# Token-major SSM operands by VectorE transposes of 32x32 squares and transfers through DRAM, in place of TensorE transposes

## The chip, the cores and the metric

The kernel runs on one core of a Trainium2 chip. The metric is the device time of one execution in microseconds; 3 timed runs of the kernel before have a median of 1086.67 us (1086.59 to 1087.11). The core has five engines that run their own instruction queues in order and wait for each other on semaphores: TensorE (PE in the profile; PEld is its weight load), VectorE (DVE), ScalarE (ACT), GpSimd (POOL) and SyncE (SP). SP and POOL also issue DMAs; 16 DMA engines carry them out.

## The reference, cut to what matters

One decoder layer on x of 512 tokens by 1024 channels, all float32: a normalised input projection, dilated attention and a Mamba-2 mixer side by side, gates, an output projection, and a squared-ReLU MLP. The change lies in the Mamba-2 mixer (8 groups, 4 heads of 64 channels each, state 128, chunks of 128 tokens):

```python
xbc = jax.nn.silu(conv(xbc) + conv_b)                 # depthwise, causal, 4 taps
xs, bm, cm = jnp.split(xbc, [SSM_INNER, SSM_INNER + SSM_GROUPS * SSM_STATE], axis=-1)
...
xd = (x * dt[..., None]).reshape(b, c, ch, g, hg, p)
cb = jnp.einsum('bclgn,bcsgn->bcgls', cc, bc)
y_diag = jnp.einsum('bcghls,bcsghp->bclghp', cb[:, :, :, None] * decay, xd)
states = jnp.einsum('bclgn,bcghl,bclghp->bcghpn', bc, decay_states, xd)
...
y_off = jnp.einsum('bclgn,bcghpn,bcghl->bclghp', cc, prev, jnp.exp(a_cs))
y = y + d_skip * xh;  y = y * silu(z);  y = y * rsqrt(mean(y * y) + eps) * norm_w   # per group
```

## The kernel before, in words

Every large matmul multiplies float32 numbers as a high and a low part (`split`, L95: ScalarE writes the high part, VectorE subtracts to get the low one), in three matmuls for each product (`three`). Weights come by SP DMAs into `ws_*`, and are split into `wh_*` and `wl_*`, two buffers of each.

The SSM stage runs over 8 groups g. For each group four kinds of projections are made as units of work that a filler hands to TensorE between the other steps: `x{g}` (PSUM tiles psx, two of 128 channels by 512 tokens), `bc{g}` (psbc: B, then C), `z{g}` (psz) and `sp{g-1}` (pssp: the projection of the group before to the model width, 8 tiles, each added to acc). After each psx or psbc tile `conv_silu` (L689) does the convolution on VectorE (ch, L693), a tanh on ScalarE (L696) and the last product on VectorE (ct, L697). The result has channels on partitions and tokens along the row.

`ssm_group` (L768) then has seven steps. In the first, x must have tokens on partitions: TensorE transposes it in eight 128x128 pieces into PSUM (ptx, through `tr`, L230), VectorE multiplies by dt into xd (L780), scales to xs, and splits it into xsh and xsl. In the second, B of the first three chunks is transposed likewise (pb) and split into bkh and bkl; TensorE multiplies B by C (pcb), VectorE masks it (cbm, L798) and multiplies the decays w (L802). The third step has the nine matmuls of the chunk states (pst, of bkh, bkl, xsh, xsl) and the running state prev. The fourth has pyd (xd and w) and pyo (prev and C) and forms y. The fifth takes the mean square of y (sq, pn, pnt, rt) and gives the row rstd to all partitions through DRAM: POOL writes rt_d (L859) and reads it back as rg (L861); it also starts the read of the next group's decays w (L754). In the last, y times nw and rg (L868) is split into yth and ytl for the projection sp{g}.

Between the steps the filler runs for a number of microseconds of TensorE work by its own count: `SSM_FILL` (L46) for groups 0 to 6, `SSM_LAST` for group 7. TensorE's instructions stand in the order of the program; those of VectorE, ScalarE, POOL and SP are put into an order by priorities, in which evacuations of projection tiles go ahead. The SSM tiles come from a pool in which tiles of one tag share buffers (sq has two, t1 two, xd one).

Of the kernel before, what the change touches and what calls it, by code (L numbers as in the profile page):

```python
# [11 lines left out]
F32 = mybir.dt.float32  # L12
F32R = mybir.dt.float32r
AF = mybir.ActivationFunctionType
ALU = mybir.AluOpType
# [3 lines left out]
P = 128  # L19
T = 512  # L20
NT = 4
# [16 lines left out]
UC = 256  # L38
# [4 lines left out]
BIG = 1e30  # L43

FILL0, FILL1, FILLA, FILLB, FILLC = 3.0, 4.0, 3.0, 2.8, 2.8
SSM_FILL = (2, 7, 4, 3, 10.5, 5, 4.5)  # L46
SSM_LAST = (3, 8, 4, 3, 9, 8, 8)

V_ORDER = tuple((d, i) for d in (1, 0, 2) for i in range(NT))
# [34 lines left out]
def hybrid_block(ctx: ExitStack, tc: tile.TileContext, a: dict):  # L84
    nc = tc.nc
    act, dve, pool, pe, sp = nc.scalar, nc.vector, nc.gpsimd, nc.tensor, nc.sync
# [5 lines left out]
    dram = ctx.enter_context(tc.tile_pool(name="dram", bufs=1, space=DRAM))  # L92


    def split(src, hi, lo, eng=None, pinned=False, lo_pinned=False):  # L95
        ins = act.activation(hi, src, AF.Copy)  # L96
        if pinned:
            tc.keep_in_program_order(ins)
        ins = (eng or dve).tensor_tensor(lo, src, hi.bitcast(F32), op=ALU.subtract)  # L99
        if lo_pinned:  # L100
            tc.keep_in_program_order(ins)
# [60 lines left out]
    def v3(t, k):  # L162
        return t.rearrange("p (k n) -> p k n", k=k)
# [65 lines left out]
    def tr(dst, src):  # L229
        tc.keep_in_program_order(pe.transpose(dst, src, ident))  # L230
# [27 lines left out]
    def abank(name):  # L258
        return psa.tile([P, T], F32, name=name, tag="a")
# [18 lines left out]
    with tc.tile_pool(name="start", bufs=1, reuse_waits="tile") as st:  # L278
# [163 lines left out]
        t = [vp.tile([P, GROUPS, NT, HG], F32, name=f"dt{j}") for j in range(4)]  # L442
# [22 lines left out]
    dtc = dtp.rearrange("p g c h -> p (g c h)")  # L465
# [50 lines left out]
    def in_unit(key, evac):  # L516

        hi, lo = take(key)
        for c in range(2):
            ps = gbank(f"ps{key}_{c}")  # L520
            yield from gemm_part(ps, v3(hi, KD), v3(lo, KD), c, range(KD), KD, uhk, ulk)
            with tc.high_priority(offset=400):
                evac(c, ps)
        done()
# [103 lines left out]
    for key in ATT_UNITS:  # L628
        n, j = key[:-1], int(key[-1])
        fill.add(key, qk_unit(n, j) if n in "qk" else z_unit(0, sz0) if n == "z" else gate_unit(n, j))  # L630
    fill.through("q0")
    pc, pa, pt = abank("pc"), abank("pa"), abank("pact")
# [51 lines left out]
    sg = sctx.enter_context(tc.tile_pool(name="ssm", bufs=1, side="right", reuse_waits="tile"))  # L684
# [4 lines left out]
    def conv_silu(ct, ps, tag, bufs):  # L689
        h = sg.tile([P, T], F32, name=f"ch{ct}", tag="ch", bufs=2)  # L690
        act.activation(h, ps, AF.Identity, bias=cb_[:, ct : ct + 1], scale=cw[:, ct, 3:4])  # L691
        for d in (1, 2, 3):
            dve.scalar_tensor_tensor(h[:, d:], ps[:, : T - d], cw[:, ct, 3 - d : 4 - d], h[:, d:],  # L693
                                     op0=ALU.mult, op1=ALU.add)
        t = sg.tile([P, T], F32, name=f"ct{ct}", tag=tag, bufs=bufs)
        act.activation(t, h, AF.Tanh)  # L696
        dve.scalar_tensor_tensor(t, t, 1.0, h, op0=ALU.add, op1=ALU.mult)  # L697
        return t

    def bc64(t, g, c0=0, c1=NT):  # L700
        v = t[:, g * 16 + c0 * HG : g * 16 + c1 * HG]
        return v.unsqueeze(2).broadcast_to([P, (c1 - c0) * HG, 64])

    def h64(ap_):
        return ap_.rearrange("p (q e) -> p q e", e=64)
# [25 lines left out]
        return evac  # L731

    convs = {}

    def x_unit(g):
        def evac(c, ps):
            convs[g, c] = conv_silu(2 * g + c, ps, "cx", 4)

        return in_unit(f"x{g}", evac)

    def bc_unit(g):
        def evac(c, ps):
            convs[g, 2 + c] = conv_silu(16 + 8 * c + g, ps, "cb" if c == 0 else "cc", 2)

        return in_unit(f"bc{g}", evac)

    TC = T - P
# [20 lines left out]
    def ssm_group(g, sz):  # L768

        xs2 = [convs.pop((g, c)) for c in range(2)]  # L770
        w, e = ws_e.pop(g)

        xd = sg.tile([P, NT * UC], F32, name=f"xd{g}", tag="xd")
        for b in range(2):
            pt = abank(f"ptx{g}_{b}")
            for c2 in range(2):
                c = 2 * b + c2
                for j, xx in enumerate(xs2):
                    tr(pt[:, c2 * UC + j * P : c2 * UC + (j + 1) * P], xx[:, c * P : (c + 1) * P])
            dve.tensor_tensor(h64(xd[:, b * T : (b + 1) * T]), h64(pt), bc64(dtc, g, 2 * b, 2 * b + 2), op=ALU.mult)  # L780
        xs = sg.tile([P, 3 * UC], F32, name=f"xs{g}", tag="prev")
        dve.tensor_tensor(h64(xs), h64(xd[:, : 3 * UC]), bc64(ds_, g, 0, 3), op=ALU.mult)
        xsp = [sg.tile([P, 3 * UC], F32R, name=f"xs{n}{g}", tag=f"xs{n}") for n in "hl"]
# [1 line left out]
        yield  # L785

        bt, ct = convs.pop((g, 2)), convs.pop((g, 3))
        pb = abank(f"pb{g}")
        for c in range(3):
            tr(pb[:, c * P : (c + 1) * P], bt[:, c * P : (c + 1) * P])  # L790
        bk = [sg.tile([P, TC], F32R, name=f"bk{n}{g}", tag=f"bk{n}") for n in "hl"]
        split(pb[:, :TC], *bk)
        pcb = abank(f"pcb{g}")
        for c in range(NT):
            cs = slice(c * P, (c + 1) * P)
# [3 lines left out]
                          op=ALU.mult)  # L799
# [21 lines left out]
        ys, sq = [], []  # L821
# [7 lines left out]
        for j in range(2):  # L829
# [6 lines left out]
            t1 = sg.tile([P, TC], F32, name=f"t1{g}_{j}", tag="t1", bufs=2)  # L836
# [46 lines left out]
    for g in range(GROUPS):  # L883
        fill.add(f"x{g}", x_unit(g))
        fill.add(f"bc{g}", bc_unit(g))
        if g == 0:
            for j in (2, 3):
                fill.add(f"ap{j}", att_unit(j))
        else:
            fill.add(f"z{g}", z_unit(g, szs[g]))  # L890
            fill.add(f"sp{g-1}", project_unit(g - 1, acc_evac(g - 1)))
# [4 lines left out]
    for g in range(GROUPS):  # L896
        steps = ssm_group(g, szs[g])
        fill.through(f"bc{g}")
        for n, us in enumerate(SSM_LAST if g == GROUPS - 1 else SSM_FILL):
            fill.run(us)  # L900
            if n == 3 and g > 0:
                fill.through(f"z{g}")
            next(steps, None)
# [361 lines left out]
    j = last  # L1265
# [106 lines left out]
```

## Time and profile before

| | |
|---|---|
| median of 3 timed runs | 1086.67 us (1086.59 to 1087.11) |
| the profiled execution | 1087.34 us |
| its span | 1085.6 us |
| instructions | 14723 |
| TensorE's mean granted clock | 0.998 |
| DMA traffic | 113.06 MB in 87654 packets, mean 104 GB/s |
| POOL's DMA queue (software_dynamic) | 2224 packets, 11.09 MB, 3.1% of 16 engines |

The span is the stretch from the first to the last instruction that the profiler recorded. In the rows, a name such as psx stands for all tiles of that kind, 128x512 is partitions by elements, and the bracket names what ended the idle time ahead of a row. Matmuls are pipelined: a row has 0.39 us, while the next one starts 0.23 us later, so times on TensorE are counted from start to start. The chain of waits is the sequence of work that ended last, followed back from the end.

The SSM stage fills the time from the first psx matmul at 243 us to the last group's sp projection, which begins at 680 us. In its middle (groups 2 to 6) each group takes 50.9 us.

### The profile page before, as it was taken

Reading aid. Unit: us, or ns where it says so; the run is one execution under the profiler, and the core shown is the slowest. Engines: PE = TensorE matmul, PEld = TensorE weight load, DVE = VectorE, ACT = ScalarE, POOL = GpSimd, SP = SyncE. Lnnn points to the kernel's source line nnn. Section 1 sums busy time; section 2 is a strip of 40 time slices with the busy share of each in tenths; the row PEclk is TensorE's granted clock in tenths of the full one; section 3 lists DMA queues with packets and bytes.
Section 4 is the critical chain, followed back from the end, with each engine's and each line's share of the span. In section 5 each row is a group of like instructions: output and inputs, shape, how many; then the busy total and the mean of one; then the engine's idle time right before and its main releaser. Section 6 shows DMA issues by size and latency. Waiting matters only on the chain.

```text
span 1085.6 us, 14723 instructions
## 1 busy us (share of the span) xinstructions
PE 1074.3 (99%) x5959; PEld 915.7 (84%) x5959; DVE 732.2 (67%) x1096; ACT 535.5 (49%) x921; POOL 72.0 (7%) x87
## 2 busy tenths in 40 slices
PE   9999999999999999999999999999999999999997
PEld 8988787778888888888888878889899998888886
DVE  6657666436777878797979795868677785242324
ACT  6356656526375645547373723454467665332222
POOL 2203122000000010100000000000000000000000
PEclk9999999999999999999999999999999999999999
DMA  8232122322433332333434223540233324333202
GB/s 276 86 100 78 59 78 68 100 76 90 134 88 117 88 126 78 126 83 122 126 103 130 88 80 124 189 160 1 78 117 117 117 80 141 110 120 114 82 35 78
DMA packets 87654, 113.06 MB, mean 104 GB/s; under 512 B 4625, under 2 KB 74769, under 8 KB 86561
## 3 DMA queue, kind: packets, MB, share of 16 engines
q1 hardware_dynamic: 85216, 101.01, 28.9%
q0 software_dynamic: 2224, 11.09, 3.1%
q8 instruction: 47, 0.77, 0.3%
q14 instruction: 23, 0.18, 0.1%
q10 hardware_dynamic: 144, 0.00, 0.0%
HBM read 109.92 MB, written 2.18 MB: 103 GB/s over the span
## 4 chain that ended last, share of the span: by engine, by line
PE 92%; DVE 4%; DMA 2%; ACT 1%; issue 1%; SPq 0%; POOL 0%; POOLq 0%; DVEq 0%; ACTq 0%
PE psd L227 16%; PE psx L227 8%; PE psz L227 8%; PE psbc L227 8%; PE pssp L227 7%; PE psuX L227 6%; PE psu L227 4%; PE psga L227 4%; PE psgs L227 4%; PE psk L227 3%; PE psq L227 3%; PE psuZ L227 3%; PE psv L227 3%; PE psap L227 3%; PE psuY L227 1%; PE pq L227 1%
## 5 line engine op out<-in xcount | busy, mean ns | idle before, releaser
L227 PE MATMUL psd<-wh_dn,hh 128*128 128x512 f32 x240 | 93.4, 389 | 0.0
L227 PE MATMUL psd<-wl_dn,hh 128*128 128x512 f32 x240 | 93.4, 389 | 0.0
L227 PE MATMUL psd<-wh_dn,hl 128*128 128x512 f32 x240 | 93.4, 389 | 0.0
L99 DVE TENSOR_TENSOR hl<-hidden,hh 128x512 fp32r<-128x512 f32 x31 | 21.1, 692 | 71.4 <-ACT hh L96 71.3
L96 ACT ACTIVATE hh<-hidden 128x512 fp32r<-128x512 f32 x31 | 19.1, 628 | 92.0 <-PE psd L227 92.0
L227 PEld LDWEIGHTS psd<-wh_dn,hl 128*128 128x128 f32 x240 | 45.0, 188 | 9.4
L227 PEld LDWEIGHTS psd<-wh_dn,hh 128*128 128x128 f32 x240 | 45.0, 188 | 9.4
L227 PEld LDWEIGHTS psd<-wl_dn,hh 128*128 128x128 f32 x240 | 45.0, 188 | 9.2
L842 ACT ACTIVATE sq<-y 128x512 f32<-128x512 f32 x16 | 17.8, 1120 | 70.5 <-DVE y L839 70.4
L227 PE MATMUL psz<-uh,wh_z 128*128 128x512 f32 x128 | 51.1, 399 | 0.0
L227 PE MATMUL pssp<-yth,wh_sp 128*128 128x512 f32 x128 | 50.9, 398 | 0.0
L227 PE MATMUL psx<-uh,wl_x 128*128 128x512 f32 x128 | 50.0, 390 | 0.7 <-DVE wl_x L99 0.7
L227 PE MATMUL psx<-uh,wh_x 128*128 128x512 f32 x128 | 50.6, 396 | 0.0
L227 PE MATMUL pssp<-yth,wl_sp 128*128 128x512 f32 x128 | 50.1, 392 | 0.0
L227 PE MATMUL psz<-uh,wl_z 128*128 128x512 f32 x128 | 50.0, 391 | 0.0
L227 PE MATMUL pssp<-ytl,wh_sp 128*128 128x512 f32 x128 | 49.9, 390 | 0.0
L227 PE MATMUL psbc<-uh,wh_bc 128*128 128x512 f32 x128 | 49.9, 390 | 0.0
L227 PE MATMUL psz<-ul,wh_z 128*128 128x512 f32 x128 | 49.9, 390 | 0.0
L227 PE MATMUL psx<-ul,wh_x 128*128 128x512 f32 x128 | 49.8, 389 | 0.0
L227 PE MATMUL psbc<-uh,wl_bc 128*128 128x512 f32 x128 | 49.8, 389 | 0.0
L227 PE MATMUL psbc<-ul,wh_bc 128*128 128x512 f32 x128 | 49.8, 389 | 0.0
L693 DVE SCALAR_TENSOR_TENSOR ch<-psx,cw,ch 128x511 f32<-128x511 f32 (+2 forms) x48 | 35.6, 742 | 20.4 <-ACT ch L691 19.7
(361 smaller groups left out, 3253.9 us busy)
## 6 DMA issues: line engine op xcount, KB each, us to landing
ws_up<-in_w_up_dram SPq DMA_DIRECT2D x16, 1024.0 KB, 5.5
ws_dn<-in_w_down_dram SPq DMA_DIRECT2D x15, 1024.0 KB, 5.0
ws_z<-in_w_in_dram SPq DMA_DIRECT2D x8, 1024.0 KB, 7.1
ws_x<-in_w_in_dram SPq DMA_DIRECT2D x8, 1024.0 KB, 5.2
w<-acs_d POOLq DMA_DIRECT2D x8, 1024.0 KB, 5.4
ws_bc<-in_w_in_dram SPq DMA_DIRECT2D x16, 512.0 KB, 4.7
ws_sp<-in_w_ssm_proj_dram SPq DMA_DIRECT2D x8, 1024.0 KB, 4.9
ws_ga<-in_w_in_dram SPq DMA_DIRECT2D x4, 1024.0 KB, 6.2
```

What stands on the lines that cost most here:

```text
L96: ins = act.activation(hi, src, AF.Copy)
L99: ins = (eng or dve).tensor_tensor(lo, src, hi.bitcast(F32), op=ALU.subtract)
L227: tc.keep_in_program_order(pe.matmul(*args, **kw))
L693: dve.scalar_tensor_tensor(h[:, d:], ps[:, : T - d], cw[:, ct, 3 - d : 4 - d], h[:, d:], op0=ALU.mult, op1=ALU.add)
L842: pin(act.activation(q.rearrange("n (j b p) -> n j b p", j=NT, b=4), y.rearrange("n (j p b) -> n j b p", j=NT, b=4), AF.Square, scale=1.0 ...
```

## The change

x and B get tokens on partitions without TensorE. `to_rows` transposes the convolved tile in 32x32 squares by one VectorE instruction (STREAM_TRANSPOSE, L741; tiles sqt and sqtb), which leaves each square in its place; four POOL DMAs (L744), one for each 32 partitions, then put the squares where they belong in a DRAM array of rows (x_d: 512 x 256, b_d: 384 x 128), in pieces of 32 floats. A further DMA reads the array back with tokens on partitions (xd, L755; br, L766). The writes and reads are issued where the tile is evacuated, ahead of the group's steps. In `ssm_group` the transposes are gone, xd is multiplied by dt in place in one instruction (L797), and B is split from br. The first two fills change from 2 and 7 to 5 and 4.

```diff
-SSM_FILL = (2, 7, 4, 3, 10.5, 5, 4.5)
+SSM_FILL = (5, 4, 4, 3, 10.5, 5, 4.5)
...
+    xrows, xds, brs = {}, {}, {}
+
+    def to_rows(src, rows_, c0, tag, name):
+        n = src.shape[-1]
+        t = sg.tile([P, n], F32, name=f"sqt{name}", tag=tag, bufs=2)
+        dve.transpose(t, src)
+        for r in range(4):
+            rs_ = slice(32 * r, 32 * r + 32)
+            pool.dma_start(rows_[:, c0 + 32 * r : c0 + 32 * r + 32].rearrange("(m i) j -> i m j", i=32),
+                           t[rs_, :].rearrange("i (m j) -> i m j", j=32))
 
     def x_unit(g):
         def evac(c, ps):
             convs[g, c] = conv_silu(2 * g + c, ps, "cx", 4)
+            if c == 0:
+                xrows[g] = dram.tile([T, UC], F32, name=f"x_d{g}")
+            to_rows(convs[g, c], xrows[g], c * P, "sq", f"{g}_{c}")
+            if c == 1:
+                xds[g] = sg.tile([P, NT * UC], F32, name=f"xd{g}", tag="xd")
+                pool.dma_start(v3(xds[g], NT), xrows[g].rearrange("(k p) j -> p k j", p=P))
...
             convs[g, 2 + c] = conv_silu(16 + 8 * c + g, ps, "cb" if c == 0 else "cc", 2)
+            if c == 0:
+                rows_ = dram.tile([TC, P], F32, name=f"b_d{g}")
+                to_rows(convs[g, 2][:, :TC], rows_, 0, "t1", f"b{g}")
+                brs[g] = sg.tile([P, TC], F32, name=f"br{g}", tag="t1", bufs=2)
+                pool.dma_start(v3(brs[g], NT - 1), rows_.rearrange("(k p) j -> p k j", p=P))
...
-        xd = sg.tile([P, NT * UC], F32, name=f"xd{g}", tag="xd")
-        for b in range(2):
-            pt = abank(f"ptx{g}_{b}")
-            for c2 in range(2):
-                c = 2 * b + c2
-                for j, xx in enumerate(xs2):
-                    tr(pt[:, c2 * UC + j * P : c2 * UC + (j + 1) * P], xx[:, c * P : (c + 1) * P])
-            dve.tensor_tensor(h64(xd[:, b * T : (b + 1) * T]), h64(pt), bc64(dtc, g, 2 * b, 2 * b + 2), op=ALU.mult)
+        xd = xds.pop(g)
+        dve.tensor_tensor(h64(xd), h64(xd), bc64(dtc, g), op=ALU.mult)
...
-        pb = abank(f"pb{g}")
-        for c in range(3):
-            tr(pb[:, c * P : (c + 1) * P], bt[:, c * P : (c + 1) * P])
         bk = [sg.tile([P, TC], F32R, name=f"bk{n}{g}", tag=f"bk{n}") for n in "hl"]
-        split(pb[:, :TC], *bk)
+        split(brs.pop(g), *bk)
```

On TensorE the order is the same but for the transposes, which are gone. On the other engines it moves at three places. The first is POOL's queue from the mean square of group 3 on, where group 4's x and B are made (rt3: the mean square, x_d4 and b_d4: the DRAM rows, w5: the next decays). Before:

```order
L215 TENSOR_TENSOR rt3_3936<-rt3_3936,mhalf_68 128x4
L859 DMA rt_d3_3939<-rt3_3936 128x4
L861 DMA rg3_3941<-rt_d3_3939 128x512
L754 DMA w5_4372<-acs_d_94 128x2048
L215 TENSOR_TENSOR rt4_4365<-rt4_4365,mhalf_68 128x4
```

and now:

```order
L215 TENSOR_TENSOR rt3_3975<-rt3_3975,mhalf_68 128x4
L873 DMA rt_d3_3978<-rt3_3975 128x4
L744 DMA x_d4_3954<-sqt4_0_3955 32x16x32 x4
L744 DMA x_d4_3954<-sqt4_1_4032 32x16x32 x4
L875 DMA rg3_3980<-rt_d3_3978 128x512
L744 DMA b_d4_4081<-sqtb4_4082 32x12x32
L755 DMA xd4_4038<-x_d4_3954 128x4x256
L744 DMA b_d4_4081<-sqtb4_4082 32x12x32 x3
L766 DMA br4_4088<-b_d4_4081 128x3x128
L777 DMA w5_4419<-acs_d_94 128x2048
```

Fourteen DMAs have come in; rg3 stands behind the eight writes of x, xd4 behind the first write of B.

The second place is VectorE in group 4, from xd to the operands of pst (xsl and bkl), where pssp3 and acc belong to the projection of group 3. Before:

```order
L780 TENSOR_TENSOR xd4_4096<-ptx4_0_4097,dtp_90 128x512
L780 TENSOR_TENSOR xd4_4096<-ptx4_1_4103,dtp_90 128x512
L782 TENSOR_TENSOR xs4_4109<-xd4_4096,ds_91 128x768
L99 TENSOR_TENSOR bkl4_4157<-pb4_4152,bkh4_4156 128x384
L798 TENSOR_TENSOR cbm4_4165<-pcb4_4160,tri_198 128x512
L99 TENSOR_TENSOR xsl4_4112<-xs4_4109,xsh4_4111 128x768
L802 TENSOR_TENSOR w4_3943<-w4_3943,cbm4_4165 128x512
L543 SCALAR_TENSOR_TENSOR sz4_1_4174<-sz4_1_4174,psz4_1_4130 128x512
```

and now:

```order
L797 TENSOR_TENSOR xd4_4038<-xd4_4038,dtp_90 128x1024
L99 TENSOR_TENSOR ytl3_4095<-y3_1_3871,yth3_4094 128x512
L799 TENSOR_TENSOR xs4_4165<-xd4_4038,ds_91 128x768
L812 TENSOR_TENSOR cbm4_4205<-pcb4_4200,tri_198 128x512
L816 TENSOR_TENSOR w4_3982<-w4_3982,cbm4_4205 128x512
L543 SCALAR_TENSOR_TENSOR sz4_1_4214<-sz4_1_4214,psz4_1_4174 128x512
L729 TENSOR_TENSOR acc0_2907<-acc0_2907,pssp3_0_4219 128x512
L99 TENSOR_TENSOR xsl4_4168<-xs4_4165,xsh4_4167 128x768
L729 TENSOR_TENSOR acc1_2916<-acc1_2916,pssp3_1_4227 128x512
L99 TENSOR_TENSOR bkl4_4197<-br4_4088,bkh4_4196 128x384
```

The second ytl stands behind xd, and bkl has moved from ahead of cbm to the end, behind w, sz, two acc and xsl. On ScalarE, the first half of wh_x and the tanh of sz now stand ahead of xsh at this place, where xsh came first before.

The third place is VectorE in group 1, from the tile of sz on (y0, ytl0: group 0's y, which the projection pssp0 reads; rg0: its row of rstd). Before:

```order
L543 SCALAR_TENSOR_TENSOR sz1_0_2832<-sz1_0_2832,psz1_0_2780 128x512
L868 SCALAR_TENSOR_TENSOR y0_0_2573<-y0_0_2573,nw_208,rg0_2687 128x512
L780 TENSOR_TENSOR xd1_2804<-ptx1_0_2805,dtp_90 128x512
L780 TENSOR_TENSOR xd1_2804<-ptx1_1_2811,dtp_90 128x512
L99 TENSOR_TENSOR ytl0_2785<-y0_0_2573,yth0_2784 128x512
L868 SCALAR_TENSOR_TENSOR y0_1_2585<-y0_1_2585,nw_208,rg0_2687 128x512
L782 TENSOR_TENSOR xs1_2817<-xd1_2804,ds_91 128x768
L99 TENSOR_TENSOR ytl0_2785<-y0_1_2585,yth0_2784 128x512
```

and now:

```order
L797 TENSOR_TENSOR xd1_2681<-xd1_2681,dtp_90 128x1024
L799 TENSOR_TENSOR xs1_2853<-xd1_2681,ds_91 128x768
L812 TENSOR_TENSOR cbm1_2889<-pcb1_2884,tri_198 128x512
L543 SCALAR_TENSOR_TENSOR sz1_1_2895<-sz1_1_2895,psz1_1_2848 128x512
L882 SCALAR_TENSOR_TENSOR y0_0_2581<-y0_0_2581,nw_208,rg0_2710 128x512
L99 TENSOR_TENSOR xsl1_2856<-xs1_2853,xsh1_2855 128x768
L99 TENSOR_TENSOR ytl0_2817<-y0_0_2581,yth0_2816 128x512
L882 SCALAR_TENSOR_TENSOR y0_1_2593<-y0_1_2593,nw_208,rg0_2710 128x512
L99 TENSOR_TENSOR bkl1_2881<-br1_2769,bkh1_2880 128x384
L816 TENSOR_TENSOR w1_2712<-w1_2712,cbm1_2889 128x512
L99 TENSOR_TENSOR ytl0_2817<-y0_1_2593,yth0_2816 128x512
```

Both y and both ytl have moved behind cbm and the second sz, and on ScalarE yth0 stands behind both halves of wh_x, where it stood ahead of them before.

## The prediction

> **What bounds the kernel now.** The page's first part says that TensorE is busy for 99% of the span, but that is a share of pipelined matmuls, so the chain of waits is read next, and there one stage: the eight SSM groups, from 243 to 680 us.
>
> ```profile
> PE 1074.3 (99%) x5959; PEld 915.7 (84%) x5959; DVE 732.2 (67%) x1096; ACT 535.5 (49%) x921; POOL 72.0 (7%) x87
> ```
>
> The chain of waits for group 4 (start us, us, what):
>
> ```profile
> 463.96 2.73 PE psz L227 x12
> 466.70 0.87 PE ptx L230 x8
> 467.57 7.51 PE psz L227 x33
> 475.08 0.33 PE pb L230 x3
> 475.40 0.89 PE pcb L227 x8
> 476.30 0.70 PE psz L227 x3
> 477.00 3.43 PE pssp L227 x15
> 480.43 1.07 PE pst L227 x9
> 481.50 2.76 PE pssp L227 x12
> ```
>
> Every piece is TensorE's and begins where the last one ends: nothing is waited for. The eight x transposes (ptx) and three B transposes (pb) are links of this chain. The same group on POOL, VectorE and ScalarE, one after the other (start, us, engine, line, tile, and the idle time before):
>
> ```profile
> 435.81 0.54 POOL L754 DMA_DIRECT2D w<-acs_d  x1 [32.24 <-PE pyo L227]
> ...
> 451.87 0.61 POOL L859 DMA_DIRECT2D rt_d<-rt  x1 [0.29 <-POOL rt L215]
> 454.14 0.55 POOL L861 DMA_DIRECT2D rg<-rt_d  x1 [1.66 <-issue]
> ```
>
> ```profile
> 449.45 0.31 DVE L854 STREAM_TRANSPOSE pnt<-pn 128x128 f32<-128x128 f32 x1
> 449.68 0.71 DVE L693 SCALAR_TENSOR_TENSOR ch<-psx,cw,ch 128x509 f32<-128x509 f32 x1
> ...
> 457.18 0.69 DVE L697 SCALAR_TENSOR_TENSOR ct<-ct,ch 128x512 f32<-128x512 f32 x1 [0.84 <-ACT ct L696]
> 459.38 1.53 DVE L693 SCALAR_TENSOR_TENSOR ch<-psbc,cw,ch 128x511 f32<-128x511 f32 x2 [1.51 <-ACT ch L691]
> ...
> 464.51 0.69 DVE L697 SCALAR_TENSOR_TENSOR ct<-ct,ch 128x512 f32<-128x512 f32 x1
> 465.11 0.75 DVE L868 SCALAR_TENSOR_TENSOR y<-y,nw,rg 128x512 f32<-128x512 f32 x1
> 465.78 0.75 DVE L693 SCALAR_TENSOR_TENSOR ch<-psbc,cw,ch 128x511 f32<-128x511 f32 x1
> 466.44 1.22 DVE L99 TENSOR_TENSOR wl_sp<-ws_sp,wh_sp 128x1024 fp32r<-128x1024 f32 x1
> 467.57 0.74 DVE L693 SCALAR_TENSOR_TENSOR ch<-psbc,cw,ch 128x510 f32<-128x510 f32 x1
> ...
> 473.08 1.28 DVE L780 TENSOR_TENSOR xd<-ptx,dtp 128x512 f32<-128x512 f32 x2
> ...
> 475.96 0.56 DVE L99 TENSOR_TENSOR bkl<-pb,bkh 128x384 fp32r<-128x384 f32 x1 [0.61 <-ACT bkh L96]
> 476.44 0.68 DVE L798 TENSOR_TENSOR cbm<-pcb,tri 128x512 f32<-128x512 f32 x1
> 477.04 0.95 DVE L99 TENSOR_TENSOR xsl<-xs,xsh 128x768 fp32r<-128x768 f32 x1
> 477.90 0.69 DVE L802 TENSOR_TENSOR w<-w,cbm 128x512 f32<-128x512 f32 x1
> ```
>
> ```profile
> 475.83 0.84 ACT L96 ACTIVATE xsh<-xs 128x768 fp32r<-128x768 f32 x1
> 476.80 1.06 ACT L96 ACTIVATE wh_x<-ws_x 128x1024 fp32r<-128x1024 f32 x1
> 477.77 0.58 ACT L542 ACTIVATE sz<-psz 128x512 f32<-128x512 f32 x1
> ```
>
> From 464.51 VectorE is a queue that runs without a gap worth naming, and its last product for pst, xsl, is there at 477.90, only 2.5 us before TensorE wants it at 480.43. So TensorE bounds the stage, with VectorE 2.5 us behind it. One VectorE instruction costs its start to the next one's start: 0.60 us for 512 columns (476.44 to 477.04), 0.66 for y and ch (465.11 to 465.78), 1.13 for 1024 (466.44 to 467.57), 0.86 for 768, 0.48 for 384, 0.23 for the 128-column transpose (449.45 to 449.68).
>
> **What the change removes.** Per group 0.87 + 0.33 = 1.20 us of TensorE; times eight, 9.6 us. That is all there is to win.
>
> **What it adds, and what hides it.** On VectorE two transposes of 512 columns and one of 384. No row shows these sizes. Bounds: 0.23 each as for 128 columns, or 0.92 and 0.69 in proportion to it; I take 0.62 and 0.50, near the other 512- and 384-column rows. The x transposes fall into idle time (the second begins after ct, at 457.78, and the next ch waits for ScalarE until 459.38), so they cost nothing; by the upper bound they still fit. The B transpose falls into the queue after 464.51. The two xd multiplies (1.20) become one of 1024 columns (1.13).
>
> On POOL, twelve writes of 512 or 384 pieces of 128 bytes and two reads per group. Let d be POOL's time for one write of an x tile, three quarters of it for a B write. The rows have 0.54 to 0.61 for DMAs over 128 partitions; d is between 0.54 (a fixed cost) and 2.4 (four times 0.61, by pieces). The ends are far apart and neither row is nearer in pieces; I take the middle in ratio, 1.2, and keep both. From issue to landing, in the view of DMA issues (KB of one, median us):
>
> ```profile
> rg<-rt_d POOLq DMA_DIRECT2D x8, 256.0 KB, 3.6
> ...
> rowe<-in_norm_ffn_post_w_dram POOLq DMA_DIRECT2D x1, 512.0 KB, 5.6
> ...
> rt_d<-rt POOLq DMA_DIRECT2D x8, 2.0 KB, 1.9
> ```
>
> Three deadlines follow. POOL takes its queue in order, and rg now stands behind the writes of the second x tile, which wait for a transpose that ends at 458.40: rg lands at 458.4 + 4d + 3.6, 466.8 for d = 1.2; its reader y is reached at 469.2 (below). The read of xd stands behind the first B write (its transpose ends at 466.74): 466.74 + 0.75d + 4.6 (between 3.6 and 5.6 by size) = 472.2; VectorE reaches xd at 472.9. The read of br follows four B writes and xd and waits for the last write, some 1.3 after its issue: 466.74 + 4d + 1.3 + 3.6 = 476.4; ScalarE reaches bkh near 477.8. So at d = 1.2 all three are hidden; above about 1.8 the first is late, and VectorE's whole queue with it.
>
> Whether VectorE's work stretches d, the trace bears on in one group of rows (duration in ns, least, median, most):
>
> ```profile
> L754 POOL DMA_DIRECT2D w<-acs_d x8: 540/543/597, 211.1 to 588.5; - x8
> ```
>
> Eight issues under a VectorE that is busy for most of each group spread by a tenth, so I add nothing for it. The Trainium skill speaks against POOL as the issuer: SBUF — State Buffer, section "A bandwidth-pool intuition that's wrong", tells of a GpSimd-issued DMA that goes from some 620 ns to some 3100 beside a VectorE copy, since its descriptors cannot be written while VectorE holds the port they share. By that figure, an estimate from that page, d would be 3.1 and all three deadlines missed; the trace does not bear it out for the work that VectorE does here.
>
> **The sum for a steady group (2 to 6).** The order shows that w, sz and two acc now stand ahead of bkl, and on ScalarE wh_x and sz ahead of xsh. VectorE from 464.51: ct 0.60, wl_sp 1.13, transpose 0.50, three ch 1.98, wl_sp 1.13, two y 1.32, sz 0.60, two ytl 1.20, ct 0.60, xd 1.13, xs 0.86, cbm 0.60, w 0.60: 12.25, so 476.76. Then sz waits for ScalarE: wh_x began 0.50 after the last three z matmuls began (476.30, 476.80); they come 1.20 earlier, so wh_x at 475.60, sz's tanh at 476.57, done at 477.1. VectorE: sz to 477.7, acc 478.3, xsl 479.16, acc 479.76, bkl 480.24. TensorE wants pst at 480.43 - 1.20 = 479.23, and its third matmul, the first that reads bkl, 0.24 later at 479.47. It starts at 480.3: 0.85 of the 1.20 is lost in a new wait for VectorE, 0.35 is kept. Five groups: -1.75 us. Groups 0 and 7 have other work beside pst; what they keep lies between 0 and 1.20 each, and I take 0.2 (the chain there runs through VectorE's steps around pst already, so less of TensorE's saving reaches the end): -0.4.
>
> **Group 1 is another case.** There y, which waits for rg, moves behind sz and cbm, and pssp, not pst, is late. The chain before, and one row each of ScalarE and VectorE:
>
> ```profile
> 315.57 7.51 PE psz L227 x33
> 323.08 0.33 PE pb L230 x3
> 323.40 0.89 PE pcb L227 x8
> 324.30 4.13 PE pssp L227 x18
> ```
>
> ```profile
> 322.88 1.06 ACT L96 ACTIVATE wh_x<-ws_x 128x1024 fp32r<-128x1024 f32 x1
> ```
>
> ```profile
> 322.89 0.69 DVE L99 TENSOR_TENSOR ytl<-y,yth 128x512 fp32r<-128x512 f32 x1
> ```
>
> Before, the second ytl was done at 323.58, ahead of pssp. After: z ends at 322.21, wh_x takes ScalarE from 322.0 to 323.0, sz's tanh and xsh to 324.2, the second half of wh_x to 325.2; only then yth. VectorE: pcb at 323.1, cbm to 323.8, sz 324.4, y 325.1, xsl 325.9, ytl 326.5, y 327.2, bkl 327.7, w 328.3, second ytl 328.9. The fifth matmul of pssp reads that; the sixth ends at 329.4 instead of 324.30 + 6 x 0.23 = 325.7. Group 1 loses 3.7 us, the 1.20 already counted.
>
> Sum: -1.75 - 0.4 + 3.7 = **+1.6 us**. The profiled execution took 1087.34 (span 1085.6 and 1.74 around it), so 1088.9 there; the median of the timed runs is 0.67 below it, 1086.67, and I forecast **1088.3**. With the transposes at their bounds (0.23 or 0.69 for B, five groups) and a microsecond either way in group 1 this case spans 1085 to 1093.
>
> **Rivals.** (a) **TensorE never waits**: the new order on VectorE does no harm, and all 9.6 us are gained: 1077.1; if half, 1082. For it: VectorE's busy share is 67%, and it has idle time before 464. Against it: in the window that matters its rows leave no gap. It decides if bkl is ready by 479.5, 0.8 us earlier than worked out. (b) **The transfers are late**: at d = 2.4 the second x tile's writes hold POOL from 458.4 to 468.0, rg lands at 471.6, four B writes and xd run to 478.2, br lands at 483.1, bkl is done near 484.0, and a steady group loses 484.1 - 479.47 - 1.20 = 3.4 us; five make 17, groups 0 and 1 by the same chain 5 and 9, group 7 one: +32, so 1118. It tips at d = 1.8. For it: a write has four times the pieces of any POOL DMA shown. Against it: POOL is 7% busy, and a 256 KB and a 2 KB DMA cost it the same. The Trainium skill's DMA: Bandwidth & Descriptors, Specifications, puts line rate at pieces of 512 bytes or more, with read-modify-write below; no row here shows such writes in number. (c) **VectorE blocks POOL**: if every POOL DMA first waits out one VectorE instruction, up to 1.22 by the wl_sp row, d is 1.2 + 1.2 = 2.4 and the time that of (b). Against it: w's 0.54. The rule of the Trainium skill's SBUF — State Buffer cited above would be this case.
>
> **Chances.** Forecast 0.47, (a) 0.20, (b) 0.28, (c) 0.05. A measurement here can tell about 0.2%, 2.2 us, from no change. The forecast lies inside that, at 0.03 faster, 0.24 same, 0.20 slower; (a) 0.16 faster, 0.04 same; (b) and (c) 0.31 slower, 0.02 same: faster 0.19, same 0.30, slower 0.51. The range takes half of (a) and (b) up to d near 2.1: 1082 to 1109.
>
> **What the profile after would show.** No ptx and pb; STREAM_TRANSPOSE rows of 512 columns near 0.7 us; POOL's x_d rows give d outright. Right: TensorE idle before pst for bkl (about 0.85 in groups 2 to 6) and before pssp in group 1 (near 6 in all). Wrong: no idle there (a), or VectorE idle before y, xd or bkl for a DMA (b, c). A transpose above 1.6 us would fill the idle time that hides the x tiles and break the sum.

## The result and the profile after

The changed kernel takes 1093.80 us (median of 4 runs, 1091.95 to 1094.37), the kernel before 1086.82 beside it: a ratio of 1.0061, 95% interval 1.0044 to 1.0079. The forecast was 1088.3, which is 1.6 above the kernel before; the range of 1082 to 1109 holds the time. The change costs 7 us, and what is to be explained is where 9.6 us of removed TensorE work went and where another 7 come from.

The first part of the page of the changed kernel (busy time, share of the span, instructions):

```profile
PE 1070.4 (98%) x5871; PEld 908.2 (83%) x5871; DVE 745.7 (68%) x1112; ACT 536.0 (49%) x921; POOL 146.1 (13%) x199
```

88 TensorE instructions are gone, 11 in each of 8 groups, as worked out. POOL's time has doubled; everything else is nearly as before. The shares say nothing of the 7 us. So the stage is cut at a mark that both kernels have, the start of pyd's first matmul in each group. The numbers below are differences of these starts, in us, from the timeline of TensorE; group g is the stretch that ends at its pyd, and for group 0 the start itself is given.

| kernel | 0 (start) | 1 | 2 | 3 | 4 | 5 | 6 | 7 | median |
|---|---|---|---|---|---|---|---|---|---|
| before | 286.08 | 46.11 | 50.22 | 50.89 | 50.89 | 50.90 | 50.89 | 53.95 | 1086.8 |
| after | 285.62 | 52.77 | 50.20 | 50.89 | 50.90 | 50.91 | 50.85 | 53.70 | 1093.8 |

Two readings. **Groups 2 to 6 take what they took** (50.2 in group 2, 50.9 in the others), to 0.04 us, though TensorE has 1.20 us less to do in each. **Group 1 takes 6.66 us more**, and that is the whole loss: with -0.46 in group 0 and -0.25 in group 7 the stage is 5.9 longer, and the span 6.1 (1091.7 against 1085.6).

A steady group first. The chain of waits of the changed kernel in group 3 (start, us, what); the chain before had nothing but TensorE here:

```profile
430.85 1.06 ACT wh_x L96
431.91 0.49 ACT sz L542
432.43 0.69 DVE sz L543
433.11 0.60 DVE acc L729
433.71 0.50 DVE xsl L99
434.50 0.68 DVE acc L729
435.18 0.48 DVE bkl L99
435.70 1.09 PE pst L227 x7
```

The chain leaves TensorE at 430.85 and comes back at 435.70: pst waits for bkl, which stands behind sz, two acc and xsl on VectorE, and sz behind wh_x on ScalarE. TensorE's timeline prices the wait, before (group 4) and after (group 3; the bracket is idle time and its releaser): the first of the last three z matmuls, the matmul of pst that reads bkl, and the first matmul behind pst.

```profile
476.05 0.48 PE L227 MATMUL psz<-uh,wh_z 128*128 128x512 f32 x1
...
480.50 0.28 PE L227 MATMUL pst<-xsh,bkl 128*128 128x256 f32 x1
...
481.34 0.39 PE L227 MATMUL pssp<-yth,wh_sp 128*128 128x512 f32 x1
```

```profile
430.10 0.48 PE L227 MATMUL psz<-uh,wh_z 128*128 128x512 f32 x1
...
434.76 0.39 PE L227 MATMUL pst<-xsh,bkh 128*128 128x256 f32 x1 [0.31 <-ACT bkh L96]
...
435.70 0.38 PE L227 MATMUL pst<-xsh,bkl 128*128 128x256 f32 x1 [0.43 <-DVE bkl L99]
...
436.63 0.39 PE L227 MATMUL pssp<-yth,wh_sp 128*128 128x512 f32 x1
```

From the z matmul to the one that reads bkl there were 4.45 us, all of them TensorE's work; now there are 5.60. And from there to the end of pst it is 0.93 and not 0.84, since the first two matmuls after the wait start 0.23 apart and not 0.12. 1.15 and 0.09: the 1.20 us are gone. That the wait is just as long as the work that was removed is a coincidence of lengths, as far as the runs below show. pst's first matmul waits too, for bkh, and ScalarE's row has the reason:

```profile
434.19 0.52 ACT L96 ACTIVATE bkh<-br 128x384 fp32r<-128x384 f32 x1 [1.06 <-DMA br<-b_d]
```

So br comes late as well. Whether its arrival or the queue on VectorE costs the 1.20 us, this trace alone does not tell.

Group 1, in the same view:

```profile
313.57 0.50 DVE sqtb L741
...
316.96 3.81 DMA b_d<-sqtb
...
321.34 5.34 DMA br<-b_d
326.70 0.53 ACT bkh L96
...
328.42 0.61 DVE ytl L99
329.08 5.55 PE pssp L227 x14
```

Here the chain runs from B's transpose through its writes, their landing, the read and its landing to bkh: 12.6 us from 314.07 to 326.70. ScalarE's timeline shows why pssp, which reads neither B nor x, waits for it:

```profile
324.66 0.62 ACT L96 ACTIVATE yth<-y 128x512 fp32r<-128x512 f32 x1
326.70 0.52 ACT L96 ACTIVATE bkh<-br 128x384 fp32r<-128x384 f32 x1 [1.43 <-DMA br<-b_d]
327.13 0.61 ACT L96 ACTIVATE yth<-y 128x512 fp32r<-128x512 f32 x1
```

bkh stands between the two yth. Both yth are late to begin with, since y waits for rg, and POOL issues rg's read behind B's four writes here, at 317.57. pssp's matmuls in TensorE's timeline:

```profile
325.33 0.50 PE L227 MATMUL pssp<-yth,wh_sp 128*128 128x512 f32 x1 [2.71 <-ACT yth L96]
326.14 0.50 PE L227 MATMUL pssp<-ytl,wh_sp 128*128 128x512 f32 x1 [0.31 <-DVE ytl L99]
...
327.80 0.79 PE L227 MATMUL pssp<-yth,wh_sp 128*128 128x512 f32 x1 [0.90 <-ACT yth L96]
329.08 0.80 PE L227 MATMUL pssp<-ytl,wh_sp 128*128 128x512 f32 x1 [0.48 <-DVE ytl L99]
329.67 0.63 PE L227 MATMUL pssp<-yth,wl_sp 128*128 128x512 f32 x1
330.10 0.63 PE L227 MATMUL pssp<-yth,wh_sp 128*128 128x512 f32 x1
```

After the waits the matmuls start 0.43 apart and not 0.23, for ten of them. The view of stretches gives the granted clock (stretch, its length, busy us of PE, PEld, DVE, ACT and POOL, then clock, DMA share, GB/s):

```profile
323.00:329.00 6.00, 2.06 (x4) 0.77 (x4) 5.49 (x10) 3.32 (x6) 0.00 (x0) 0.81 0.36 99
329.00:335.00 6.00, 5.92 (x19) 4.78 (x20) 1.83 (x4) 1.53 (x3) 0.00 (x0) 0.62 0.01 3
```

The clock was 0.62 in the six us after the wait, so group 1 pays for the wait a second time. The Trainium skill's TensorE: Matmul & The Clock Gate, section "What's actually happening", has the array at half rate after an idle window of some 3.4 us, and the section "Wait — 56ns, not 53.3ns?" gives 426.7 ns between starts there for 512 columns. The pace agrees with these rows. The time does not: the longest idle time here was 2.71 us, and four matmuls stood between the waits.

Last, the writes (POOL's time in ns, least, median, most) and the landings (KB each, median us from issue), in the views of line 744 and of DMA issues:

```profile
L744 POOL DMA_DIRECT2D x_d<-sqt x64: 648/651/697, 256.5 to 619.7; - x64
L744 POOL DMA_DIRECT2D b_d<-sqtb x32: 615/618/633, 265.0 to 628.6; - x32
```

```profile
x_d<-sqt POOLq DMA_DIRECT2D x64, 64.0 KB, 2.5
...
b_d<-sqtb POOLq DMA_DIRECT2D x32, 48.0 KB, 5.3
```

d is 0.65, near its lower bound, and B's writes, the smaller ones, land more than twice as late as x's.

### The profile page after: what moved, and what is told of

It is laid out like the page before. It is cut to its first block, busy times and chain, and to the rows that moved or that the text cites. A ratio compares the mean times of both kernels' runs of the same rounds, so it can differ in the third digit from the quotient of the medians.

```text
span 1091.7 us, 14792 instructions
## 1 busy us (share of the span) xinstructions
PE 1070.4 (98%) x5871; PEld 908.2 (83%) x5871; DVE 745.7 (68%) x1112; ACT 536.0 (49%) x921; POOL 146.1 (13%) x199
## 4 chain that ended last, share of the span: by engine, by line
PE 83%; DVE 7%; DMA 4%; ACT 4%; issue 2%; POOL 1%; POOLq 0%; SPq 0%; DVEq 0%; ACTq 0%
PE psd L227 15%; PE psx L227 7%; PE psbc L227 6%; PE psuX L227 6%; PE psz L227 6%; PE pssp L227 5%; PE psu L227 4%; PE psga L227 4%; PE psgs L227 4%; PE psk L227 3%; PE psq L227 3%; PE psuZ L227 3%; PE psv L227 3%; PE psap L227 2%; PE psuY L227 1%
## 5 line engine op out<-in xcount | busy, mean ns | idle before, releaser
L744 POOL DMA_DIRECT2D x_d<-sqt x64 | 41.5, 655 | 83.6 <-DVE sqt L741 81.7
```

What stands on the lines that cost most here:

```text
L744: pool.dma_start(rows_[:, c0 + 32 * r : c0 + 32 * r + 32].rearrange("(m i) j -> i m j", i=32), t[rs_, :].rearrange("i (m j) -> i m j", j=32))
```

## The experiments

Theory: x's half of the change is free and worth its 0.87 us per group; B's half is not, because its trip through DRAM (writes, landing, read, landing) is longer than the time that the group has for it. In the steady groups that shows as pst's wait for bkl; in group 1 as ScalarE's wait at bkh, behind which yth and pssp are late, and then as the lower clock. Rivals: VectorE or the transfers as a whole bound the stage, so that any saving of TensorE is eaten; or the loss in group 1 has nothing to do with a clock. The change of SSM_FILL to (5, 4) is no suspect: the two numbers have one sum, and with (2, 7) put back the order of instructions on every engine is that of the changed kernel, since nothing of TensorE is left between the two steps. Every ratio below is to the kernel before, timed beside the run.

### The halves apart: x_alone and b_alone

```diff
--- x_alone (B's writes and read are taken out as well)
+        pb = abank(f"pb{g}")
+        for c in range(3):
+            tr(pb[:, c * P : (c + 1) * P], bt[:, c * P : (c + 1) * P])
-        split(brs.pop(g), *bk)
+        split(pb[:, :TC], *bk)
--- b_alone (the writes and the read of x are taken out as well)
-        xd = xds.pop(g)
-        dve.tensor_tensor(h64(xd), h64(xd), bc64(dtc, g), op=ALU.mult)
...
+                    tr(pt[:, c2 * UC + j * P : c2 * UC + (j + 1) * P], xx[:, c * P : (c + 1) * P])
```

> The x half of the change without the B half: B goes through TensorE as before. First theory (the x transposes are free on VectorE, and what eats the gain is B's place in VectorE's order and B's trip through DRAM): pst does not wait, each steady group takes 50.9 - 0.87 = 50.0 us, group 1 has no long wait, and the median is 1086.7 - 8 x 0.87 = 1079.7 (1079 to 1082). Rival (VectorE or the x transfers bound the stage as soon as TensorE gets shorter): the groups stay near 50.9 and the median is 1086 or more.

> The B half of the change without the x half: x goes through TensorE as before, so no read of xd stands among B's writes, and bkl stands ahead of sz and the acc additions on VectorE. First theory: B's writes land in about 2.5 us, pst does not wait, 0.33 us per group is kept, 1084.0 (1083.5 to 1085.5). Rival (B's round trip through DRAM is too long whatever stands beside it): ScalarE waits at bkh in group 1, the clock drops there, and the time is 1087 to 1093.

x_alone takes **1081.24 us** (ratio 0.9948, 0.9935 to 0.9960), as the theory had it: 5.9 faster than before. Its groups: 284.81, then 46.07, 49.32, 49.99, 50.43, 50.00, 50.39, 53.07. No pst waits; two of the steady groups take 0.4 more than 50.0, since pyd waits for w. So of the 7.0 us that x's transposes cost on TensorE 5.9 are gained: VectorE's transposes of 512 columns, the eight writes and the read of xd cost next to nothing, and VectorE bounds the stage by no more than that 0.4.

b_alone takes **1090.42** (1.0031, 1.0020 to 1.0043). The theory's number, 1084.0, fell, and the rival's time came, but not at the place that it named: group 1 is fine (45.74) and the steady groups are slower, 52.88, 51.40, 50.54, 51.57 for groups 3 to 6. POOL's timeline in group 4, and a row of ScalarE's:

```profile
468.81 2.48 POOL L744 DMA_DIRECT2D b_d<-sqtb  x4 [12.65 <-DVE sqtb L741]
474.40 0.76 POOL L760 DMA_DIRECT2D br<-b_d  x1 [3.11 <-DMA b_d<-sqtb]
```

```profile
478.09 0.53 ACT L96 ACTIVATE bkh<-br 128x384 fp32r<-128x384 f32 x1 [2.70 <-DMA br<-b_d]
```

With no x traffic beside it B's trip still takes 9.3 us from its first write to bkh: 2.5 of issues, 3.1 until the read may go, 3.7 for the read. ScalarE stands 2.7 us at bkh, with xsh, sz and wh_x behind it, and the chain of waits there goes from br through bkh, xsh, sz and acc to xsl and pst. 0.33 us of TensorE was bought with a wait of 2.7. The Trainium skill's DMA: Bandwidth & Descriptors, section "Anatomy of one DMA", puts a fixed time of some 2 us on each DMA, most of it until the write is confirmed; the trace agrees, since the least landing of line 744 in the changed kernel was 2.0. A trip through DRAM has two landings, one after the other.

### The clock: keep_clock

```diff
+        if g == 1:
+            wm = abank("keep")
+            for _ in range(25):
+                mm(wm, uh[:, 0, 0:P], uh[:, 1, :], start=True, stop=True)
```

> The changed kernel with 25 matmuls of 512 columns more on TensorE in group 1, in the wait ahead of pssp; their result is used by nobody. No other instruction moves. First theory (after the wait the granted clock is lower, and ten pssp matmuls run 0.43 us apart and not 0.23): those matmuls run 0.23 apart, pst of group 1 comes 2.0 to 2.3 us earlier, and the median is 1091.6 (1091 to 1092.3). Rival (the slow matmuls wait for operands or for VectorE): no gain, 1093.5 or more.

**1092.33** (1091.25 to 1092.60), against 1093.80 for the changed kernel: more work and, in the median, less time. The chain of group 1, and the granted clock of the stretch after the wait:

```profile
322.94 5.70 PE keep L227 x25
328.65 4.11 PE pssp L227 x18
332.76 1.07 PE pst L227 x9
```

```profile
329.00:335.00 6.00, 6.00 (x32) 5.05 (x31) 2.93 (x7) 2.18 (x4) 0.00 (x0) 1.00 0.00 0
```

18 matmuls of pssp take 4.11, 0.23 apart, and the clock is 1.00. pst comes at 332.76 and not 334.62, 1.9 earlier (a little under the 2.0 expected). Group 1 takes 50.54 where it took 52.77, but 0.36 of that is a later start (285.98 against 285.62). The changed kernel's own rows give nearly the same: from the fifth matmul of pssp to pst it has 5.38 us from start to start (329.08 to 334.46), the kernel before 3.20 (325.07 to 328.27). So some 2 us of group 1's loss, 1.9 by the run and 2.2 by the rows, are the clock. The medians differ by 1.5, also less than expected, and their intervals overlap (1.0034 to 1.0062 here); the pace of the rows carries this reading, the medians only go along.

### B's traffic: xd_by_act, b_by_sync and rg_by_sync

The edits put one transfer each into another queue.

```diff
--- xd_by_act
-                pool.dma_start(v3(xds[g], NT), ...
+                act.dma_start(v3(xds[g], NT), ...
--- b_by_sync
-                to_rows(convs[g, 2][:, :TC], rows_, 0, "t1", f"b{g}")
+                to_rows(convs[g, 2][:, :TC], rows_, 0, "t1", f"b{g}", sp)
...
-                pool.dma_start(v3(brs[g], NT - 1), ...
+                sp.dma_start(v3(brs[g], NT - 1), ...
--- rg_by_sync
-        pool.dma_start(row, rt)
+        sp.dma_start(row, rt)
-        pool.dma_start(rstd, ...
+        sp.dma_start(rstd, ...
```

> The changed kernel with the read of xd issued by ScalarE's queue instead of POOL's, so that it does not stand among the writes of B. In the steady groups VectorE's order is that of the changed kernel, bkl behind sz, two acc and xsl. First theory (VectorE's order bounds the steady groups, the transfers bound group 1): b_d lands in about 2.5 us instead of 5.3, steady groups stay at 50.9, group 1 loses 2 to 4 us less, median 1089 to 1092. Rival (the transfers of B bound the steady groups too): their period falls by 0.3 us or more, and the median is under 1088.5.

> The changed kernel with B's four writes and its read issued by SyncE's queue instead of POOL's. In group 1 y and ytl come ahead of cbm on VectorE and yth ahead of wh_x on ScalarE, since rg is no longer behind B's writes; in groups 2 to 6 bkl keeps its place. First theory (group 1 loses by y's place and by ScalarE's wait at bkh, and then by the lower clock; the steady groups by bkl's place and arrival): group 1 falls from 52.8 to 46 to 48.5, groups 2 to 6 stay at 50.7 to 50.9, median 1088.5 (1087 to 1090). Rival (in group 1 B's trip through DRAM itself is what pst waits for, and a queue shared with the weights makes it longer): group 1 stays above 51 and the median above 1092.

> The changed kernel with the write of rt_d and the read of rg issued by SyncE's queue; B's writes and read stay on POOL. In group 1 y comes ahead of cbm on VectorE and yth ahead of wh_x and bkh on ScalarE, as in b_by_sync. First theory (group 1 loses by the place of y and yth behind a wait for B, not by the length of B's trip as such): group 1 takes 46 to 47, no pssp matmul runs at the lower clock, median 1086.5 (1086 to 1087.5). Rival (B's trip through DRAM by POOL is too long for group 1 in any order): pst waits for bkh there, group 1 takes 49 or more, median 1089 or more.

xd_by_act takes **1094.23** (1.0064, 1.0051 to 1.0077), no gain: group 0 ends 1.4 later (287.06), group 1 takes 52.26, the steady groups 50.88 to 50.90. In group 1 ScalarE still waits 1.39 us for br at bkh, and the second yth stands behind it, now at 328.51. The writes of B land in 4.4 and not in 2.5: the read of xd among them in POOL's queue explains 0.9 of the 2.8 us at most. Without any x traffic, in b_alone, they landed in 2.7; in rg_by_sync, where the read of rg is out of the queue and that of xd is not, in 4.0. Whether they are kept by what stands ahead of them in the queue or by what is transferred beside them was not separated.

b_by_sync takes **1086.27** (0.9995, 0.9986 to 1.0004), as long as before and 2 us under what was expected. Group 1 takes 46.10: all of its loss is gone. The chain of its group 1:

```profile
322.89 0.61 DVE ytl L99
...
323.55 3.51 PE pssp L227 x14
```

Groups 2 to 6 stay at 50.20 to 50.90, as expected, and here the trace tells more than the time. The two rows for group 3, bkh on ScalarE and bkl on VectorE:

```profile
426.40 0.51 ACT L96 ACTIVATE bkh<-br 128x384 fp32r<-128x384 f32 x1
```

```profile
427.52 0.55 DVE L99 TENSOR_TENSOR bkl<-br,bkh 128x384 fp32r<-128x384 f32 x1
```

ScalarE does not wait for br at all, in none of the groups 2 to 6, and yet bkl starts 46.50 us behind the pyd of the group before (381.02), as in the changed kernel (435.09 less 388.59). xd_by_act has the same 46.50 (436.02 less 389.52). So the place in VectorE's queue holds the steady groups by itself; in the changed kernel br's late arrival is hidden behind it.

rg_by_sync, which leaves B on POOL, takes **1087.09** (1.0002, 0.9993 to 1.0011), group 1 46.28. B's trip is still long there, 10.8 us from its transpose to bkh (314.33 to 325.13; 12.6 in the changed kernel), and it does no harm. So B's trip as such is not what group 1 loses by. In both kernels the read of rg is issued ahead of B's writes or from another queue, the order has y and both yth ahead of bkh, as in the kernel before, and pssp can start; B then lands under pssp's 18 matmuls. The loss of group 1 was **what stood in front of yth**, a wait for a transfer that pssp does not need.

### The deadline and the place of bkl: pst_later, both_fixes, bk_ahead, both_from_1

```diff
--- pst_later (and both_fixes, with b_by_sync's edit)
-SSM_FILL = (5, 4, 4, 3, 10.5, 5, 4.5)
+SSM_FILL = (5, 4, 6, 3, 8.5, 5, 4.5)
--- bk_ahead
-        split(xs, *xsp)
+        with tc.high_priority(offset=400 if g > 1 else 0):
+            split(xs, *xsp)
...
-        split(brs.pop(g), *bk)
+        with tc.high_priority(offset=400 if g > 1 else 0):
+            split(brs.pop(g), *bk)
--- both_from_1 (with b_by_sync's edit)
+        ... (5, 4, 6, 3, 8.5, 5, 4.5) if g else SSM_FILL
```

> The changed kernel with the filler's third number 6 and its fifth 8.5 (before 4 and 10.5): nine matmuls of pssp stand ahead of pst on TensorE that stood behind it, so the deadline of bkl is 2 us later; nothing is added or taken away. First theory (in groups 2 to 6 pst waits because B's products come at a fixed time, about 10 us after its transpose, and the queue behind it adds to that): the wait is gone, the groups fall from 50.9 to 49.7 (up to 50.2), group 1 stays at 52.8, median 1088 (1086.5 to 1089.5). Rival (VectorE as a whole bounds a group, so any later place fills up too): the groups stay at 50.9 and the median at 1092.5 or more.

> The two edits of pst_later and b_by_sync together. If the two losses are apart, as the first theory has it, their gains add: groups 2 to 6 near 49.7, group 1 near 47, median 1082.5 (1080 to 1084.5), faster than before. If VectorE or the transfers bound the stage, 1087 or more.

> The changed kernel with xsh, xsl, bkh and bkl given a higher priority in groups 2 to 7: in these, xsl and bkl stand ahead of sz and of the second acc on VectorE, and xsh ahead of sz on ScalarE. Group 1 keeps its order. If the place in VectorE's queue is what pst waits for, sz and acc (1.2 us) leave the path, the groups fall to 49.7 and the median to 1088 (1087 to 1089). If the arrival of br bounds them as well (ScalarE waits 1.0 to 1.4 us for it at bkh in the changed kernel's trace), bkl can start at bkh's end only, 0.4 to 0.5 earlier than now: groups near 50.4, median 1091.5 (1090.5 to 1092.3).

> both_fixes with the filler's numbers of group 0 left as they are, so that only groups 1 to 6 have pst later. If pst_later lost its gain in group 0 alone (there psx came ahead of its weights, waited 2.8 us for wl_x and then ran at the lower clock), group 0 ends near 284.7 as in b_by_sync, groups 2 to 6 take 50.3, and the median is 1082.6 (1081.8 to 1083.6). If the moved work is waited for in group 1 or 2 just as well, 1085 or more.

pst_later takes **1094.27** (1.0070, 1.0057 to 1.0082): half a miss. Groups 3 to 6 fall to 50.3 and the wait of pst for bkl is gone from them, but group 0's pyd starts at 292.62, 7.0 later, of which 2 are work moved forward. Waits of TensorE (us in total, times, longest):

```profile
PE pn L227 <- DVE sq L860: 2.9, 5, 0.6
PE psx L227 <- DVE wl_x L99: 2.8, 1, 2.8
```

In group 0 psx now comes ahead of its weights, waits 2.8 and runs its next 13 matmuls 0.43 apart. In the steady groups pn waits 0.6 for sq, so that half of the 1.2 us is kept there. both_fixes takes **1086.10** (0.9993, 0.9985 to 1.0002), not 1082.5: it loses in group 0 too (289.24, with the same wait of 2.8 for wl_x). both_from_1 leaves group 0 alone and takes **1082.85** (0.9961, 0.9948 to 0.9975), inside what was expected; its group 0 ends at 285.16, and groups 3 to 6 take 50.3. Group 1 takes 48.79, 2.7 more than in b_by_sync: 2 are again work moved forward, and 0.7 was not followed up. That settles where pst_later lost, and that a later deadline does free the steady groups.

bk_ahead takes **1100.76** (1.0124, 1.0109 to 1.0139), and both theories fell. VectorE's timeline in group 3, and TensorE's longest wait in total:

```profile
435.54 0.56 DVE L99 TENSOR_TENSOR bkl<-br,bkh 128x384 fp32r<-128x384 f32 x1 [0.91 <-ACT bkh L96]
...
437.69 0.69 DVE L818 TENSOR_TENSOR w<-w,cbm 128x512 f32<-128x512 f32 x1
```

```profile
PE pyd L227 <- DVE w L818: 5.9, 13, 0.8
```

bkl, put ahead, has to wait 0.9 us for br, and VectorE waits with it. sz and acc are then done later, w behind them, and pyd waits for w. Groups 3 to 6 take 52. In the changed kernel two bounds fell together, the place in the queue and the arrival of br: for groups 3 to 6 b_by_sync moved the arrival alone and bk_ahead the place alone, and neither made them shorter. And in bk_ahead what was taken out of the path came back in front of pyd.

### How much is free: refill

```diff
+        if 2 <= g <= 6:
+            wm = abank(f"keep{g}")
+            for _ in range(5):
+                mm(wm, uh[:, 0, 0:P], uh[:, 1, :], start=True, stop=True)
```

> b_by_sync with five matmuls of 512 columns more ahead of pst on TensorE in each of groups 2 to 6 (25 in all, 25 x 0.227 = 5.7 us of TensorE; their result is used by nobody); no other instruction moves. First theory (in these groups the whole 1.20 us that the transposes left is a wait for bkl now, so as much work fits in for nothing): the groups stay at 50.9, the wait of pst for bkl is gone from the trace, median 1086.3 (1085.9 to 1087.0). Rival (the wait is only a shift, and TensorE still bounds the group over its whole length): each group takes 1.1 us more, median 1092.

**1086.31** (0.9993, 0.9985 to 1.0002) against b_by_sync's 1086.27: 5.7 us of matmuls cost nothing, and pst no longer waits in groups 2 to 6. The chain of group 3:

```profile
423.30 3.42 PE pssp L227 x15
426.73 1.13 PE keep L227 x5
427.86 1.21 PE pst L227 x9
```

The five matmuls stand where the transposes' time had become a wait. At this place in groups 2 to 6 TensorE's time had no price any more, up to the 1.1 us per group that were put in.

### A better version: x_alone_tuned

```diff
+        ... (5, 4, 4, 4, 9.5, 5, 4.5) if g > 1 else SSM_FILL
```

> x_alone with the filler's fourth number 4 and its fifth 9.5 from group 2 on (before 3 and 10.5): four or five more matmuls of pssp stand between pst and pyd, so w has 1 us more. In x_alone every second steady group takes 50.4 and not 50.0, with pyd waiting 0.4 for w. First theory: that wait goes, all steady groups take 50.0, median 1080.3 (1079.7 to 1081.0). Rival (as in pst_later, what is moved is waited for elsewhere): 1081.2 or more.

**1082.15** (0.9955, 0.9941 to 0.9968), 0.9 above x_alone with an interval that overlaps x_alone's: no gain, as the rival had it. Groups 1 to 7 add up to 349.8, x_alone's to 349.3; pyd still waits for w in groups 4 and 6, and in 3 and 5 the chain of waits runs through the norm's sq. x_alone, 1081.24, stays the fastest of all kernels here, faster than before and after.

## Why the prediction came out as it did

The sign of the forecast's sum, +1.6, was right and its size was not; the profiled span grew by 6.1. The time lies in the stated range because that range was made wide for rival (b), which did not come; the forecast's own span, 1085 to 1093, ends 0.8 below the 1093.80 measured. The signs named for the profile after were there: TensorE idle before pst for bkh and bkl in groups 2 to 6, against rival (a), and in group 1 before and within pssp (2.71, 0.31, 0.90 and 0.48, in all 4.4 where near 6 was forecast). By its own steps:

- **What the change removes**: 1.20 us per group, 88 instructions, as worked out.
- **VectorE's transposes**: taken at 0.62 and 0.50 from the rows near in columns. Right; the rows show 0.71 and 0.57 of busy time, and 0.50 from sqtb's start to the next in the chain.

```profile
L741 DVE STREAM_TRANSPOSE sqt<-ct 128x512 f32<-128x512 f32 x16 | 11.4, 710 | 0.4
L741 DVE STREAM_TRANSPOSE sqtb<-ct 128x384 f32<-128x384 f32 x8 | 4.6, 572 | 0.0
```

- **d**: taken at 1.2 between 0.54 and 2.4, measured 0.65, and three quarters for B was wrong too (0.62). Four times the pieces cost POOL about a tenth more. The middle between far bounds was too high; the lower bound, from rows that were shown, was the better one. It did no harm, since 1.8 was the point of decision. Rivals (b) and (c) fell by the places that they named: no write waits for VectorE (648 to 697 ns for 64 of them). The 3.1 us that the Trainium skill's SBUF — State Buffer, section "A bandwidth-pool intuition that's wrong", gives for a GpSimd-issued DMA beside a VectorE copy are not seen in any of them. VectorE's rows beside these writes are operations of two inputs and transposes; no run has copies in their place.
- **The three deadlines**: those of rg and xd were met in the steady groups. That of br failed, by a term that stood in one clause: the landing of the last B write was taken at 1.3 us, and no row carried that. It was 5.3 in the median. In group 4 ScalarE reached bkh 1.39 before br was there. It cost a steady group nothing, by b_by_sync. The late transfer that rival (b) forecast was real, with another cause than the one it was priced by.
- **The steady group**: order and times of VectorE were right, and its queue is the bound, as forecast. The prediction had bkl done at 480.24; the stage of the changed kernel runs 6.2 later by then, and there the next instruction started at 486.45. The term of 0.35 kept was mis-sized, since measured it is 0.0. Three small parts make it up. The time at which TensorE wants pst was read from the chain of waits, 480.43, while its timeline has pst start at 480.27 (0.16). The matmul that reads bkl started 0.1 later than worked out. And pst is 0.1 slower behind a wait. That is 1.75 us over five groups.
- **Group 1**: the step that was too small. The second ytl was worked out for 328.9, and the instruction behind it started at 328.94. But +3.7 should have been +6.7. The fifth matmul of pssp started 4.0 later than before (329.08 against 325.07), 0.3 more than worked out. From there to pst the matmuls were counted at 0.23 each and ran at 0.43: 2.2 more. The last 0.46 is what group 0 had gained: group 1 started earlier by that, and its wait did not end earlier. The term left out was the clock. The prediction had the wait of 6 us in its sum and never asked what TensorE would do after it.
- **Groups 0 and 7**: -0.2 each, measured -0.46 and -0.25. These two were a guess between 0 and 1.20, and no run looked into them.

The difference between sum and profile is group 1 (3.0) and the steady groups (1.7), less 0.3 for groups 0 and 7.

## What to carry to other kernels

Work that moves from a busy engine into a trip through DRAM needs slack for two landings in a row and for what is beside them, here 9 to 13 us; x had it, B had not, so split such a change and keep the half that has. What a saved microsecond becomes is read at the next wait: if it turns into a wait for another engine, as much work fits in free there, and the gain comes only when that engine's product or its deadline is moved. And an instruction that waits for a transfer on an in-order engine delays everything behind it, so look at what stands behind the waiting one (yth here) before looking at what it feeds; and ask of a wait on TensorE of some us what the clock does after it (here waits of 4.4 us in all cost 2 us more).

## What was not expected of the hardware

- The granted clock fell to 0.62 although no idle time was longer than 2.71 us: TensorE was busy 2.06 of the 6 us from 323 to 329. Ten matmuls then started 0.43 apart. In pst_later one idle time of 2.81 us, with matmuls 0.23 apart ahead of it, was followed by 13 matmuls 0.43 apart.
- A DMA write of 512 pieces of 128 bytes costs POOL 0.65 us to issue, DMAs over 128 partitions (rg, w, rt_d) 0.57 to 0.61. SyncE issued the writes of B, 0.62 on POOL, in 0.48 (median of 0.33 to 0.75, in b_by_sync), and ScalarE the read of xd, 0.78 on POOL, in 0.37 (in xd_by_act).
- B's writes of 48 KB landed in 2.7 us with nothing of x beside them, in 4.0 with the read of rg out of POOL's queue, in 4.4 with that of xd out of it, and in 5.3 with both in it.
- After a wait the first two of pst's matmuls of 256 columns start 0.23 apart and the others 0.12, which makes a wait 0.1 us dearer than its length.
